# Four turned value tiles keep their store buffer in dead rows of the start stage instead of the result ring

## The chip, the core and the metric

The kernel runs on one core of one Trainium2 chip. The metric is the device time of one execution in microseconds (us). Matrix products run on TensorE (PE in the profile), vector work on VectorE (DVE), casts and activations on ScalarE (ACT), small work and a part of the transfers on GpSimd (POOL). SyncE (SP) only issues transfers.

## The reference, cut to what matters

One decoder layer on 1024 tokens with 1024 channels: a normalised and modulated input `h`, one wide projection, windowed attention and a gated recurrence side by side, and a merge.

```
h = rmsnorm(x, norm_g) * (1 + scale) + shift
proj = h @ w_in
q_a, k_a, v_a, z_a, q_b, f_b, i_b, z_b, g_a, g_b = split(proj)
o_a = dilated_attention(heads(q_a), heads(k_a), heads(v_a), rel_bias) * silu(z_a)   # 8 heads of 64
o_b = rmsnorm(hgrn2(silu(q_b), f_b, i_b, lb)) * silu(z_b)
y = sigmoid(g_a) * (o_a @ w_branch_a) + sigmoid(g_b) * (o_b @ w_branch_b)
out = rmsnorm(x + gate * (y @ w_out), final_g)
```

The change touches the values `v_a` of heads 2 and 3. The projection leaves them with channels on partitions; attention wants them with tokens on partitions.

## The kernel before

Every product is split in three (high by high, low by high, high by low part); `mm3` (L240 to L243) records the three matmuls. `split` (L245) makes the parts of a weight piece: a cast on ACT (`w_hi`, L248) and a difference on DVE (`w_lo`, L226).

**The stream.** The projection is a list of steps, each of which prepares one piece of weights (128 x 4 x 128 floats, 256 KB) and runs twelve matmuls on it. Two column blocks together are done as seven products of sums of blocks (`add_pair`): the steps in order take the pieces `i11`, a sum, a second sum, a third sum, `i12`, a difference, `i22`. A step's parts are prepared two steps ahead (`AHEAD`). The attention of head 0 begins while the stream still runs; its score and value steps are put between the products.

**The pieces.** Each piece is loaded by SP (L260) into one of eight slots, `w_raw0` to `w_raw7`. Slots 6 and 7 belong to a pool (`wraw2`) that opens only when the start stage has closed; they lie where the start stage had `xt0`. A slot gets a new piece when the old one has been split.

**The ring.** Results wait for their stores in a ring of six tiles `ct` of 128 x 512 (`ctile`, pool `ctp`). A seventh tile must wait until the store of an earlier one has landed.

**The turned values.** `ev_v(p)` takes the values of heads 2p and 2p+1 out of PSUM into a `ct` and, two or three steps later, turns them: PE transposes four blocks into `pt` (L452), ACT casts the high part into a `ct` (L456), DVE subtracts to get the low part (L226), and SP stores the tile (L458) to `vq_d` in memory. Each p has two halves of tokens and two tiles in each, so four stores of 256 KB. p = 0 and p = 1 are turned close together, where the start stage ends.

**The attention's loads.** POOL loads a head's half of `toep`, `qp`, `k1`, `k2` (L903, L909) and its turned values `vq` (L914). In head 0 the second half's loads are held back by four one-element copies on POOL (L901, L902) that read the last turned tile of p = 0.

**What sets the order.** PE's order is that of the code. ACT, DVE and POOL follow the code up to `region.close()`; behind it, and on SP throughout, the scheduler places an instruction by when what it needs is free in its plan. Each engine then works strictly in its order. `start` (with the input blocks `xt0` and `xt1` of 128 x 8 x 512) lies on the right of the on-chip memory; when it closes, the attention's tiles take its place.

Of the kernel before, what the change touches and what calls it, by code (L numbers as in the profile page):

```python
# [10 lines left out]
F32 = mybir.dt.float32  # L11
F32R = mybir.dt.float32r
# [7 lines left out]
P = 128  # L20
S = 1024
D = 1024
KT = D // P
# [156 lines left out]
def hybrid_layer(ctx: ExitStack, tc: tile.TileContext, x, w_ada, b_ada, w_in, w_branch_a, w_branch_b, w_out,  # L180
                 rel_bias, final_g, smalls, consts, onehot, logc, out, tap=None):
    nc = tc.nc
    ctx.enter_context(tc.manual_schedule(engines={mybir.EngineType.PE}))

    cpool = ctx.enter_context(tc.tile_pool(name="cpool", bufs=1))
# [14 lines left out]
    nc.gpsimd.memset(ones, 1.0)  # L200
    ident = kc[:, K_ID:K_ID + P]
    lbt = cpool.tile([P, 6, 8], F32, name="lbt")
    mx_, e0, e1, lb, oml, tm = (lbt[:, n] for n in range(6))


# [19 lines left out]
    def sub(out_, a, hi):  # L225
        nc.vector.tensor_tensor(out_, a, hi.bitcast(F32), ALU.subtract)  # L226
# [37 lines left out]
    def ctile(dt=F32):  # L264
        return ctp.tile([P, 512], dt, name="ct")
# [123 lines left out]
    def half_of(th):  # L389
        return slice(512 * th, 512 * th + 512)  # L390

    def as_ct(src, psum):
        if not psum:
            return src
        t = ctile()
        nc.scalar.copy(t, src)
        return t
# [42 lines left out]
    def ev_k(p):  # L440
        return ev_split(4 * p + 2, 1.0)

    turned, last_v = {}, {}

    def ev_v(p, wait=2):
        def ev(src, th, psum):
            t = as_ct(src, psum)

            def turn():
                pt = pools["t"].tile([P, 4, P], F32, name="pt")  # L450
                for n in range(4):
                    nc.tensor.transpose(pt[:, n], t[:, n * P:(n + 1) * P], ident)  # L452
                for n in (0, 2):
                    vs = ctile(F32R).rearrange("p (a h e) -> p a h e", a=2, h=2)
                    got = pt[:, n:n + 2].rearrange("p a (h e) -> p a h e", h=2)
                    nc.scalar.copy(vs[:, :, :, 0:E], got)  # L456
                    sub(vs[:, :, :, E:P], got, vs[:, :, :, 0:E])
                    nc.sync.dma_start(vq_d[p][:, 4 * th + n:4 * th + n + 2], vs.bitcast(F32))  # L458
                    last_v[p] = vs
                turned["v", p] = turned.get(("v", p), 0) + 1  # L460
            stream.after(wait, turn)
        return ev
# [58 lines left out]
    with ExitStack() as st:  # L521
        px = st.enter_context(tc.tile_pool(name="ps_x", bufs=1, space=PSUM))
        pm = st.enter_context(tc.tile_pool(name="ps_main", bufs=1, space=PSUM))
        xt = [sp.tile([P, KT, 512], F32, name=f"xt{th}") for th in range(2)]
# [141 lines left out]
        def first_products(j, ths=(0, 1), us=(0, 1, 2)):  # L666
            for th in ths:
                bh, bl = X[NAMES[j // 4, th]]
                k = j % 4
                for u in us:  # L670
                    hi, lo = firsts[u + 3 * (j // 4)]
                    nc.tensor.matmul(main[u, th], hi[:, k], bh[:, k], start=j == 0, stop=False)
                    nc.tensor.matmul(main[u, th], lo[:, k], bh[:, k], start=False, stop=False)
                for u in us:
                    nc.tensor.matmul(main[u, th], firsts[u + 3 * (j // 4)][0][:, k], bl[:, k], start=False,
                                     stop=j == KT - 1)

        def block_sum(name, c):

            s, u = slice(2 * c, 2 * c + 2), slice(2 * c + 4, 2 * c + 6)  # L680
            to, a, b_ = {"t1": (xt[0][:, s], xt[1][:, s], xt[0][:, s]), "t3": (xt[1][:, s], xt[1][:, u], xt[1][:, s]),
                         "t2": (xt[0][:, s], xt[1][:, u], xt[0][:, s]),
                         "t4": (xt[0][:, u], xt[0][:, u], xt[0][:, s])}[name]
            hi, lo = X[name]
            return [lambda: nc.vector.tensor_tensor(to, a, b_, ALU.subtract),
                    lambda: nc.scalar.copy(hi[:, s], to), lambda: sub(lo[:, s], to, hi[:, s])]
# [4 lines left out]
        def tick(another=True):  # L691

            if sums and another:
                under_way.append(block_sum(*sums.pop(0)))
            for parts in under_way:
                parts.pop(0)()
            while under_way and not under_way[0]:
                under_way.pop(0)
# [142 lines left out]
        tick()  # L841
        first_products(KT - 1, us=(0,))
        stream.ahead(0, 1)
        tick()
        for th in range(2):
            FIRST[0][1](main[0, th], th, True)
# [25 lines left out]
    with ExitStack() as at:  # L872
# [7 lines left out]
        def load_head(h):  # L880
            p = h // 2
            if p > 0:
                stream.need(f"qk{p}")
            while turned.get(("v", p)) != 2:
                stream.step()
            qp, k1, k2 = ([ap1.tile([P, 512], F32R, name=f"{n}{c}") for c in range(2)] for n in ("qp", "k1", "k2"))
            toep = ap1.tile([P, S], F32, name="toep")
            heads[h] = qp, k1, k2, toep, [None, None]
            load_half(h, 0)
            if h == 0:  # L890
                load_half(h, 1)
            load_value(h, 0)

        def load_half(h, c):


            qp, k1, k2, toep, _ = heads[h]
            if h == 0 and c == 1:
                got = last_v[0][:, 0, 0, 0:1].bitcast(F32)
                for t in (qp[1], k1[1], k2[1]):  # L900
                    nc.gpsimd.tensor_copy(t[:, 0:1], got)  # L901
                nc.gpsimd.tensor_copy(toep[:, 512:513], got)  # L902
            nc.gpsimd.dma_start(toep[:, half_of(c)],  # L903
                                bass.AP(tensor=toep_d.tensor, offset=toep_d.offset + h * TOEP + 512 * c,
                                        ap=[[1, P], [1, 512]]))
            p, r = h // 2, slice(E * (h % 2), E * (h % 2) + E)
            for dst, n in ((qp, 4 * p), (k1, 4 * p + 2), (k2, 4 * p + 3)):
                for hh in range(2):
                    nc.gpsimd.dma_start(dst[c][E * hh:E * hh + E],  # L909
                                        qk_d[n + hh if dst is qp else n][r, half_of(c)].bitcast(F32R))  # L910
# [60 lines left out]
        def begin(n):  # L971

            if n < len(items):
                h, j = items[n]
                rows[n] = []
                for i in (2 * j, 2 * j + 1):
                    rows[n].append(score(h, i))
                    if i == 1:
                        if h > 0:
                            load_half(h, 1)  # L980
                        load_value(h, 1)
                    if i == 7 and h + 1 < NH:
                        load_head(h + 1)
                    yield
# [519 lines left out]
```

## Time and profile before

| what | us |
|---|---|
| median of three executions (1118.89 to 1120.88) | 1120.68 |
| profiled execution, its own time | 1119.58 |
| its span, first to last instruction | 1117.70 |
| PE busy | 1093.9 |
| DVE busy | 807.4 |
| ACT busy | 554.9 |

Times in the views are counted from the first instruction. The start of a row and its duration overlap with the next row's, since instructions are pipelined; what matters is the distance from start to start. The place of this change lies between 83 us (where the first transposes of values stand) and 119 us.

### The profile page before, as it was taken

How to read it: one execution, taken by the hardware profiler on the slowest of the kernel's cores; microseconds unless marked ns; L12 is line 12 of the kernel's file. 1: busy time of each engine (PE TensorE's matmuls, PEld its weight loads, DVE VectorE, ACT ScalarE, POOL GpSimd, SP SyncE). 2: the span in 40 equal slices, each digit the busy share in tenths (PEclk: the TensorE clock that was granted, in tenths of full speed). 3: DMA queues.
4: the chain of work that ended last, by engine and by line, in shares of the span. 5: the costliest groups of instructions: out<-in, count | busy, mean ns of one | idle time of the engine just before them, and what ended most of it. 6: DMA issues, size and time to landing. Idle time of an engine off the chain costs nothing.

```text
span 1117.7 us, 21827 instructions
## 1 busy us (share of the span) xinstructions
PE 1093.9 (98%) x8302; PEld 905.0 (81%) x8302; DVE 807.4 (72%) x1607; ACT 554.9 (50%) x1144; POOL 124.0 (11%) x207
## 2 busy tenths in 40 slices
PE   8998999999999999999999999999999999999997
PEld 6687888888888888888887888878887888888886
DVE  5586988878777776854788898897977773769053
ACT  6564656687555555632455554555554443334021
POOL 1112202203203201100000000000010012000000
PEclk9999999999999999999999999999999999999999
DMA  9849567637636624856625354453534379854052
GB/s 311 265 126 244 170 180 189 175 104 179 161 102 169 156 73 148 268 164 211 225 86 180 104 191 129 137 165 92 188 124 154 130 263 351 267 187 138 13 189 75
DMA packets 161608, 189.54 MB, mean 170 GB/s; under 512 B 11440, under 2 KB 107824, under 8 KB 161504
## 3 DMA queue, kind: packets, MB, share of 16 engines
q1 hardware_dynamic: 140080, 153.95, 43.1%
q0 software_dynamic: 21024, 33.60, 12.3%
q8 instruction: 65, 1.06, 0.4%
q10 hardware_dynamic: 400, 0.61, 0.2%
q14 instruction: 39, 0.32, 0.1%
HBM read 129.36 MB, written 58.76 MB: 168 GB/s over the span
## 4 chain that ended last, share of the span: by engine, by line
PE 79%; DVE 8%; DMA 6%; issue 3%; ACT 2%; POOL 1%; DVEq 0%; POOLq 0%; SPq 0%; ACTq 0%
PE m L241 17%; PE m L243 16%; PE m L242 16%; PE po L959 3%; PE pt L944 3%; PE pq L241 3%; PE pq L243 2%; PE pq L242 2%; PE pp L1125 2%; DMA gbr<-gb_d 2%; DVE w_lo L226 2%; PE pss L927 1%; PE pss L926 1%; DMA ld<-in_w_ada_dram 1%; PE pou L1221 1%
## 5 line engine op out<-in xcount | busy, mean ns | idle before, releaser
L226 DVE TENSOR_TENSOR w_lo<-w_raw,w_hi 128x512 fp32r<-128x512 f32 x156 | 106.9, 687 | 59.4 <-ACT w_hi L248 59.0
L248 ACT CAST w_hi<-w_raw 128x512 fp32r<-128x512 f32 x146 | 90.5, 621 | 43.7 <-PE m L243 29.2
L248 ACT CAST w_hi<-w_s 128x512 fp32r<-128x512 f32 x90 | 55.9, 621 | 56.6 <-PE m L243 37.9
L330 ACT COPY ct<-m 128x512 f32<-128x512 f32 x90 | 52.7, 585 | 58.4 <-PE m L243 48.8
L277 DVE TENSOR_TENSOR ct<-m,ct 128x512 f32<-128x512 f32 x90 | 61.8, 687 | 23.9 <-PE m L243 23.6
L226 DVE TENSOR_TENSOR w_lo<-w_s,w_hi 128x512 fp32r<-128x512 f32 x90 | 61.8, 687 | 11.7 <-ACT w_hi L248 10.6
L932 ACT ACTIVATE s<-s,st 128x128 f32<-128x128 f32 (+3 forms) x64 | 49.8, 778 | 33.0 <-DVE st L929 33.0
L948 ACT CAST pth<-pt 128x512 fp32r<-128x512 f32 (+1 forms) x80 | 43.5, 544 | 34.0 <-PE pt L944 29.7
L1229 POOL TENSOR_TENSOR ssh<-ssh,halfh 128x4 f32<-128x4 f32 x16 | 19.5, 1216 | 332.9 <-DVE ssh L1228 332.8
L226 DVE TENSOR_TENSOR ptl<-pt,pth 128x512 fp32r<-128x512 f32 (+1 forms) x80 | 50.6, 632 | 7.4 <-ACT pth L948 6.6
L241 PE MATMUL m<-t3h,w_hi 128*128 128x512 f32 x120 | 49.5, 412 | 2.2 <-ACT w_hi L248 2.2
L241 PE MATMUL m<-b22h,w_hi 128*128 128x512 f32 x124 | 50.9, 410 | 0.0
L241 PE MATMUL m<-b11h,w_hi 128*128 128x512 f32 x124 | 50.9, 410 | 0.0
L241 PE MATMUL m<-b21h,w_hi 128*128 128x512 f32 x124 | 50.6, 408 | 0.0
L241 PE MATMUL m<-t4h,w_hi 128*128 128x512 f32 x120 | 49.5, 412 | 1.1 <-issue 0.5
L242 PE MATMUL m<-b22h,w_lo 128*128 128x512 f32 x124 | 48.6, 392 | 1.8 <-issue 1.8
L241 PE MATMUL m<-t2h,w_hi 128*128 128x512 f32 x120 | 49.2, 410 | 0.7 <-ACT ct L330 0.7
L241 PE MATMUL m<-t1h,w_hi 128*128 128x512 f32 x120 | 49.4, 412 | 0.3 <-DVE ct L277 0.3
L243 PE MATMUL m<-b21l,w_hi 128*128 128x512 f32 x124 | 48.6, 392 | 0.0
L242 PE MATMUL m<-b11h,w_lo 128*128 128x512 f32 x124 | 48.6, 392 | 0.0
L243 PE MATMUL m<-b11l,w_hi 128*128 128x512 f32 x124 | 48.6, 392 | 0.0
L243 PE MATMUL m<-b22l,w_hi 128*128 128x512 f32 x124 | 48.6, 392 | 0.0
(365 smaller groups left out, 3226.6 us busy)
## 6 DMA issues: line engine op xcount, KB each, us to landing
w_raw<-in_w_in_dram SPq DMA_DIRECT2D x128, 256.0 KB, 3.5
wa<-in_w_ada_dram SPq DMA_DIRECT2D x16, 512.0 KB, 9.2
qk_d<-ct SPq DMA_DIRECT2D x32, 256.0 KB, 3.1
k<-qk_d POOLq DMA_DIRECT2D x64, 128.0 KB, 5.2
toep<-toep_d POOLq DMA_DIRECT2D x16, 256.0 KB, 5.5
qp<-qk_d POOLq DMA_DIRECT2D x32, 128.0 KB, 5.1
vq_d<-ct SPq DMA_DIRECT2D x16, 256.0 KB, 3.9
vq<-vq_d POOLq DMA_DIRECT2D x16, 256.0 KB, 4.3
```

Source lines behind the costliest of these rows:

```text
L226: nc.vector.tensor_tensor(out_, a, hi.bitcast(F32), ALU.subtract)
L241: nc.tensor.matmul(ps, ah, bh, start=start, stop=False, skip_group_check=more)
L242: nc.tensor.matmul(ps, al, bh, start=False, stop=False, skip_group_check=more)
L243: nc.tensor.matmul(ps, ah, bl, start=False, stop=stop, skip_group_check=more)
L248: nc.scalar.copy(hi, src)
L277: nc.vector.tensor_tensor(out_, a, b_, op)
L330: nc.scalar.copy(c[name], b[which])
L932: nc.scalar.activation(s[:, :kw], s[:, :kw], AF.Exp, bias=prev, scale=-1.0, accum_out=st2[:, 2:3])
L944: nc.tensor.transpose(pt[:, c0:c0 + P], pn[b][:, kt * P:(kt + 1) * P], ident)
L948: nc.scalar.copy(pth[:, :w], pt[:, :w])
L959: nc.tensor.matmul(po[:, 256 - n:256], vq[kt // 4][:, kt % 4], src[:, c0:c0 + n], start=kt == 0 and a == 0, stop=kt == 2 * j + 1 and a == 1)
L1125: nc.tensor.matmul(to[:, 0], k_[:, o:o + 32], q_[:, o:o + 32], start=True, stop=True)
```

## The change

The four tiles of p = 1 (heads 2 and 3) are no longer `ct` tiles. They use rows 4 to 7 of `xt1`, the second half's input block, which nothing reads any more at that place. And the element that POOL's four copies read is first copied to a tile of its own, `came`, by one DVE instruction, so that the ring tile isn't read by POOL.

```diff
+    came = cpool.tile([P, 16], F32, name="came")[:, 0:1]
...
                 for n in (0, 2):
-                    vs = ctile(F32R).rearrange("p (a h e) -> p a h e", a=2, h=2)
+                    vs = vs_free.pop(0).bitcast(F32R) if p == 1 else ctile(F32R)
+                    vs = vs.rearrange("p (a h e) -> p a h e", a=2, h=2)
...
-                    last_v[p] = vs
+                    if p == 0 and (th, n) == (1, 2):
+                        nc.vector.tensor_copy(came, vs[:, 0, 0, 0:1].bitcast(F32))
...
         stream.ahead(0, 1)
+        vs_free.extend(xt[1][:, n] for n in range(4, KT))
...
-                got = last_v[0][:, 0, 0, 0:1].bitcast(F32)
                 for t in (qp[1], k1[1], k2[1]):
-                    nc.gpsimd.tensor_copy(t[:, 0:1], got)
-                nc.gpsimd.tensor_copy(toep[:, 512:513], got)
+                    nc.gpsimd.tensor_copy(t[:, 0:1], came)
+                nc.gpsimd.tensor_copy(toep[:, 512:513], came)
```

The lines behind the first edit move by one to four. PE's order is the same before and after. On the other engines rows move. A tile's number at its end counts up in the program; the same piece has a number smaller by two in the changed program (`w_raw7_976` before is `w_raw7_974` after: slot 7, the piece `i11` with which the next pair of column blocks begins).

On SP, from the last stores of the first keys on, before:

```order
L260 DMA w_raw6_974<-in_w_in_dram 128x4x128
L260 DMA w_raw7_976<-in_w_in_dram 128x4x128
L458 DMA vq_d_97<-ct_856 128x512
L458 DMA vq_d_97<-ct_860 128x512
L458 DMA vq_d_97<-ct_869 128x512
L458 DMA vq_d_97<-ct_873 128x512
L458 DMA vq_d_97<-ct_922 128x512
L458 DMA vq_d_97<-ct_926 128x512
L458 DMA vq_d_97<-ct_935 128x512
L458 DMA vq_d_97<-ct_939 128x512
L260 DMA w_raw2_982<-in_w_in_dram 128x4x128
L260 DMA w_raw3_984<-in_w_in_dram 128x4x128
```

and after, at the same place:

```order
L460 DMA vq_d_98<-ct_857 128x512
L460 DMA vq_d_98<-ct_861 128x512
L460 DMA vq_d_98<-ct_870 128x512
L460 DMA vq_d_98<-ct_874 128x512
L460 DMA vq_d_98<-xt1_119 128x512 x4
L261 DMA w_raw2_980<-in_w_in_dram 128x4x128
L261 DMA w_raw3_982<-in_w_in_dram 128x4x128
L261 DMA w_raw4_984<-in_w_in_dram 128x4x128
L261 DMA w_raw6_972<-in_w_in_dram 128x4x128
L261 DMA w_raw7_974<-in_w_in_dram 128x4x128
```

The two loads of slots 6 and 7 stood ahead of all eight stores and now stand behind them, as the last of five loads; the load of slot 7 also waits for the first store out of `xt1` to have landed, the third of the five waits for the DVE low part of slot 4 (`w_lo_961<-w_raw4_603`).

On DVE, where the pieces of the running pair are used up and the first scores of head 0 begin, before:

```order
L226 TENSOR_TENSOR w_lo_944<-w_raw2_598,w_hi_943 128x512
L277 TENSOR_TENSOR w_raw4_602<-w_raw3_600,w_raw4_602 128x512
L929 ISA s0_1028,st2_1029<-pss_1030,toep_1007 128x128
L929 ISA st2_1029 128x1
L226 TENSOR_TENSOR w_lo_963<-w_raw4_602,w_hi_962 128x512
L933 RECIPROCAL st2_1029<-st2_1029 128x1
L929 ISA s0_1043,st2_1044<-pss_1045,toep_1007 128x256
```

and after:

```order
L278 TENSOR_TENSOR w_raw4_603<-w_raw3_601,w_raw4_603 128x512
L227 TENSOR_TENSOR w_lo_961<-w_raw4_603,w_hi_960 128x512
L278 TENSOR_TENSOR w_raw0_976<-w_raw7_974,w_raw0_976 128x512
L227 TENSOR_TENSOR w_lo_1062<-w_raw7_974,w_hi_1061 128x512
L933 ISA s0_1026,st2_1027<-pss_1028,toep_1005 128x128
L933 ISA st2_1027 128x1
L937 RECIPROCAL st2_1027<-st2_1027 128x1
L938 TENSOR_SCALAR s0_1026<-s0_1026,st2_1027 128x128
L933 ISA s0_1041,st2_1042<-pss_1043,toep_1005 128x256
```

Two operations on slot 7 (`w_raw7_974`) now stand ahead of the first score's minimum (`s0_1026<-pss`), where before it needed no load of that kind.

On ACT, at the same place, before:

```order
L248 CAST w_hi_943<-w_raw2_598 128x512
L330 COPY ct_959<-m2_882 128x512
L248 CAST w_hi_962<-w_raw4_602 128x512
L932 ACTIVATE s0_1028,st2_1029<-s0_1028,st2_1029 128x128
L248 CAST w_hi_1063<-w_raw7_976 128x512
```

and after:

```order
L249 CAST w_hi_941<-w_raw2_599 128x512
L331 COPY ct_957<-m2_884 128x512
L249 CAST w_hi_960<-w_raw4_603 128x512
L249 CAST w_hi_1061<-w_raw7_974 128x512
L936 ACTIVATE s0_1026,st2_1027<-s0_1026,st2_1027 128x128
```

The cast of slot 7 changed places with the first exponential of head 0. On POOL the four copies now read `came`, and the first load of turned values (`vq`) moved from behind the second half's seven loads of `toep`, `qp` and `k` to ahead of them.

More of the change, by code (lines that the diff above doesn't have):

```diff
@@ L441, in ev_k @@
         return ev_split(4 * p + 2, 1.0)
-    turned, last_v = {}, {}
+    turned, vs_free = {}, []
     def ev_v(p, wait=2):
```

## The prediction

> **What bounds the kernel now.** I read the page first.
>
> ```profile
> span 1117.7 us, 21827 instructions
> PE 1093.9 (98%) x8302; PEld 905.0 (81%) x8302; DVE 807.4 (72%) x1607; ACT 554.9 (50%) x1144; POOL 124.0 (11%) x207
> ```
>
> PE is busy for all but 24 us, so only time in which PE stands still, or starts again late, can be won or lost. Next the chain that ended last, between 60 and 126 us (start, length, what):
>
> ```profile
> 90.92 0.59 ACT ct L330
> ...
> 93.83 7.71 DMA vq_d<-ct
> 101.65 0.59 ACT ct L330
> ...
> 118.65 0.38 PE pss L926
> ```
>
> and the waits between 80 and 125 us (us in total, times, longest):
>
> ```profile
> ACT ct L330 <- DMA vq_d<-ct: 4.9, 1, 4.9
> PE m L241 <- ACT w_hi L248: 2.2, 1, 2.2
> ACT ct L456 <- DMA vq_d<-ct: 1.8, 2, 1.5
> PE m L241 <- ACT ct L330: 0.7, 1, 0.7
> ```
>
> The copy of a product into the ring at 101.65 waits for the fifth store of turned values (the first of heads 2 and 3), which takes 7.71 us to land. From there the chain goes over ACT and DVE, and is back on PE only at 118.65. PE's timeline prices the stall (start, length, [idle before it]):
>
> ```profile
> 83.46 1.03 PE L452 MATMUL pt<-kc,ct 128*128 128x128 f32 x8
> 84.25 0.48 PE L241 MATMUL m<-b11h,w_hi 128*128 128x512 f32 x1
> 89.81 1.04 PE L452 MATMUL pt<-kc,ct 128*128 128x128 f32 x8
> 91.56 0.50 PE L241 MATMUL m<-t2h,w_hi 128*128 128x512 f32 x1 [0.71 <-ACT ct L330]
> 100.18 0.39 PE L243 MATMUL m<-b21l,w_hi 128*128 128x512 f32 x1
> 102.81 0.49 PE L241 MATMUL m<-t3h,w_hi 128*128 128x512 f32 x1 [2.24 <-ACT w_hi L248]
> 106.20 0.49 PE L944 MATMUL pt<-kc,s 128*128 128x128 f32 x3
> ...
> 114.43 0.48 PE L926 MATMUL pss<-k,qp 128*128 128x512 f32 x1
> ```
>
> **What the change removes.** Two PE stalls. First, the eight transposes at 83.46 are followed by the next product after 0.79 us; those at 89.81 only after 1.75 us, because the copy at 90.92 waits for the first store to land. SP's queue shows why that is late:
>
> ```profile
> 86.02 0.94 SPq L260 DMA_DIRECT2D w_raw<-in_w_in_dram  x2
> 87.06 9.97 SPq L458 DMA_DIRECT2D vq_d<-ct  x8
> 97.50 6.37 SPq L260 DMA_DIRECT2D w_raw<-in_w_in_dram  x3
> ...
> vq_d<-ct SPq DMA_DIRECT2D x1, 256.0 KB, 3.8
> ```
>
> (The last row is the issue list of 87 to 87.3 us: the first store takes 3.8 us, so it lands at 90.9.) With the two loads of 86.02 gone from ahead of it, it goes out some 0.7 us earlier and alone, and the product follows at 89.81 + 0.79 = 90.60: 0.96 us won. Second, the product that ends at 100.41 (100.18 and the 0.23 from one start to the next) would be followed at once by the twelve matmuls on t3, 12 x 0.23 = 2.75 us, which now end at 106.20: 106.20 - 100.41 - 2.75 = 3.04 us won, since the ring copy no longer waits for a store of heads 2 and 3. Together 4.0: PE would come to the transposes of the first scores (L944) at 102.2 and not at 106.20.
>
> **What it adds in work.** The copy to `came` is one DVE instruction on one column; nearest is a reciprocal of one column, 0.15 us (below). It stands ahead of the sums that feed the product at 90.6, whose low part has about 0.3 us to spare, so I take 0, and 0.15 at most. POOL's four copies begin after it instead of after the cast, half a us later. The `vq` load that now leads POOL's queue has to wait for two stores; what it delays, the second half of `qp` and `k`, is first used by the scores at 114.43. I take 0 for both.
>
> **What it moves, and the new wait.** The load of slot 7 is the last of five, and ahead of the first score DVE now has two operations on it, ACT one. Both engines work in order. So both stop until that load has landed (call this L), and PE stops at L944, whose input is the normalised first score. DVE and ACT rows for what must follow L:
>
> ```profile
> 96.26 0.42 DVE L226 TENSOR_TENSOR ct<-pt,ct 128x256 fp32r<-128x256 f32 x1 [0.44 <-ACT ct L456]
> 96.78 0.69 DVE L226 TENSOR_TENSOR w_lo<-w_raw,w_hi 128x512 fp32r<-128x512 f32 x1
> 97.39 0.69 DVE L277 TENSOR_TENSOR w_raw<-w_raw,w_raw 128x512 f32<-128x512 f32 x1
> 97.99 0.28 DVE L929 CUSTOM_DVE_ANT_0 s<-pss,toep 128x128 f32<-128x128 f32 x1
> 102.78 0.69 DVE L226 TENSOR_TENSOR w_lo<-w_raw,w_hi 128x512 fp32r<-128x512 f32 x1 [4.50 <-ACT w_hi L248]
> 103.39 0.15 DVE L933 RECIPROCAL st<-st 128x1 f32<-128x1 f32 x1
> 103.47 0.40 DVE L929 CUSTOM_DVE_ANT_0 s<-pss,toep 128x256 f32<-128x256 f32 x1
> 105.86 0.34 DVE L934 TENSOR_SCALAR s<-s,st 128x256 f32<-128x256 f32 x1
> ...
> 102.65 0.40 ACT L932 ACTIVATE s<-s,st 128x128 f32<-128x128 f32 x1
> 104.08 0.51 ACT L932 ACTIVATE s<-s,st 128x256 f32<-128x256 f32 x1
> ```
>
> After L: difference and low part 0.6 each (96.78 to 97.39 to 97.99), minimum 0.3, exponential with its sum 0.5, reciprocal and scaling 0.45, second minimum 0.4, second exponential 0.6, reciprocal and scaling 0.5, and some 0.25 between engines: 4.2 us. L944 starts at L + 4.2 against 106.20, a difference of L - 102.0. DVE's order then still holds two operations of 0.6 (a low part and a scaled result) that before were done by 106.2; as the chain runs over DVE until 118.65, PE gets its next free run 1.2 us later still, a difference of L - 100.8. I take the middle, L - 101.4. Behind 118.65 the chain is PE alone, so the difference stays to the end.
>
> **How late is L?** From below: the third of the five loads waits for the DVE low part of slot 4. Before, DVE's last turned value is done at 96.7; the casts waited 1.8 us for stores, of which some 1.2 come off, since DVE's other work stands between: 95.5, followed by cast and low part of slot 2 (1.2), the difference and cast of slot 4 (1.0) and its low part (0.6): 98.3. Two more issues at 0.4 each put the last load at 99.1, and the fastest landing in this stretch was 2.9:
>
> ```profile
> DMA to landing us min/median/max: 2.9/3.8/8.9
> DMA to landing us min/median/max: 7.9/8.4/8.9
> 90.00:92.00 2.00, 1.29 (x10) 1.01 (x9) 1.02 (x2) 1.08 (x3) 2.00 (x5) 1.00 1.08 340
> q0 software_dynamic: 390, 0.52, 109.7%
> ```
>
> (First row: loads of pieces, 80 to 125 us. Second: the two of them issued at 97.50 and 98.10. Third: the stretch 90 to 92 us, its last number GB/s. Fourth: the only queue that moved data from 94.3 to 96.5 us.) So L is at least 102.0. From above: the two loads issued at 97.50 and 98.10 sat behind four stores and beside POOL's loads and landed after 7.9 and 8.9 us, at 105.4 and 107.0. In the changed kernel two loads stand at that place too, issued within a us of it, and three more follow. At 340 GB/s 256 KB take 0.77 us, three 2.3: L = 109.3. Between these lies the wait of the last load for the first store out of `xt1`: if that lands like its predecessor, at 93.83 + 7.71 = 101.5, the load goes out then, and with nothing ahead of it lands at 101.5 + 0.4 + 2.9 = 104.8. I take 109, because the row of loads behind the same four stores is the nearest. The sum is 109 - 101.4 = 7.6 us slower: 1119.58 + 7.6 = 1127.2 for the profiled execution, and from the median, which lies 1.10 above it, 1128.3.
>
> [...]
>
> **The clock.** PE would stand still from 102.2 to 113. Before, it stood still in parts of 20 to 24 us:
>
> ```profile
> 20.00:24.00 4.00, 2.32 (x9) 1.16 (x10) 2.50 (x7) 3.30 (x6) 0.00 (x0) 0.98 1.02 402
> 24.00:28.00 4.00, 4.00 (x11) 2.76 (x11) 3.96 (x11) 3.48 (x7) 0.17 (x1) 0.59 1.08 357
> ```
>
> The granted clock (third from the end) then was 0.59 for 4 us, a loss of up to 0.41 x 4 = 1.6 us. After the new stall DVE leads, so I take 0 and keep 1.6 for the upper end. [...]
>
> **Rivals.** (1) *The queue drains sooner.* The two early loads are no longer in the way, POOL's loads start later, and only the wait for the first `xt1` store counts: L between 103.5 and 106, about 104.8, and the sum is 3.4, a time of 1124.1. [...] Against it: 7.9 and 8.9 us in the same place. (2) *The load is nearly in time.* L between 102.0 and 103.5: between 0.6 and 2.1 slower, about 1122.0, the stall of the ring paid back by the stall of the load. It needs the first `xt1` store to land by about 99, in 5.5 us, where its predecessor took 7.71. (3) *Faster.* If the last load landed by 98, before DVE needs it, nothing is left but the relief: 4.0 us won, 1116.7. It decides at L = 101.4 and shows beyond noise at 99.2. It needs the third load to be released some 3 us earlier than 98.3; the casts and differences ahead of it, 0.6 each, hardly leave that. A kernel of this kind can be told from an unchanged one by about 0.2%, 2.2 us.
>
> **How the numbers follow.** Last of a full queue (L from 106 to 111): 0.63. Rival 1: 0.21. Rival 2: 0.09. Rival 3: 0.07. The forecast is the first, 1128.3. Slower by over 0.2% (L above 103.6) is the first two, 0.84; within 0.2% rival 2, 0.09; faster 0.07. For the range, L = 102.8 gives 1.4 and 1122.0 at the lower end; L = 110.5 with the clock's 1.6 gives 10.7 and 1131.4 at the upper, which leaves out rival 3, most of rival 2 and a few in a hundred above.
>
> **What would show it.** In the changed kernel: no ACT ring copy (L331) waits for a store near 101; PE's product after the second eight transposes starts near 90.6 and the t3 product ends near 102; then DVE's difference of slot 7 (L278) and ACT's cast (L249) wait for a `w_raw` load until about 109, and PE's transposes of scores (L948) start some 4 us later, with a lower granted clock behind them. I am wrong if that load lands by 102, or if DVE and PE catch up behind the stall.

## The result and the profile after

The changed kernel takes 1125.66 us (median of five, 1123.59 to 1126.79) against 1119.93 for the kernel before in the same runs (1116.81 to 1120.88): a ratio of 1.0052, 95% interval 1.0037 to 1.0066, so 5.7 us slower. The prediction was 1128.3, range 1122.0 to 1131.4. The profiled execution shown here took 1124.04 us. Where the diff added lines, a line's number has moved by one to four (L226 is L227, L277 is L278, L926 is L930, L944 is L948).

The page, and the waits between 80 and 125 us (us in total, times, longest):

```profile
span 1122.2 us, 21825 instructions
PE 1094.3 (98%) x8302; PEld 906.5 (81%) x8302; DVE 807.6 (72%) x1608; ACT 554.8 (49%) x1144; POOL 124.1 (11%) x207
```

```profile
ACT w_hi L249 <- DMA w_raw<-in_w_in_dram: 9.1, 1, 9.1
PE pt L948 <- DVE s L938: 8.4, 2, 7.3
DVE w_raw L278 <- DMA w_raw<-in_w_in_dram: 8.3, 1, 8.3
```

PE's busy time is the same to 0.4 us, and the span grew by 4.5. No ring copy waits for a store any more. In its place ACT and DVE wait for one load of a weight piece, and PE waits for DVE. The chain that ended last says which load (start, length, what):

```profile
99.76 0.50 SPq L261
...
100.31 6.69 DMA w_raw<-in_w_in_dram
...
107.08 0.63 ACT w_hi L249
```

It is the last of five, and it landed at 107.0. PE's timeline (start, length, [idle before it]):

```profile
83.68 1.04 PE L453 MATMUL pt<-kc,ct 128*128 128x128 f32 x8
...
90.03 1.03 PE L453 MATMUL pt<-kc,ct 128*128 128x128 f32 x8
90.81 0.48 PE L242 MATMUL m<-t2h,w_hi 128*128 128x512 f32 x1
...
99.59 0.39 PE L242 MATMUL m<-t3h,w_hi 128*128 128x512 f32 x1
...
102.09 0.39 PE L244 MATMUL m<-t3l,w_hi 128*128 128x512 f32 x1
109.82 0.45 PE L948 MATMUL pt<-kc,s 128*128 128x128 f32 x1 [7.35 <-DVE s L938]
111.29 0.69 PE L948 MATMUL pt<-kc,s 128*128 128x128 f32 x2 [1.02 <-DVE s L938]
...
124.59 0.38 PE L930 MATMUL pss<-k,qp 128*128 128x256 f32 x1
```

Both stalls of the ring are gone: the products on t2 and t3 follow without a gap. PE gets to the score transposes (L948) at 102.3, and stands there until 109.82.

To compare the place alone, and not what the start stage or the later stages do in one execution or another, I use one distance from here on, D: from the first eight transposes of values to the score product 256 wide that ended the chain before (83.46 to 118.65 in the kernel before: 35.19 us). Here it is 124.59 - 83.68 = 40.91, which is 5.72 more, as much as the medians differ (5.73).

### The profile page after: what moved, and what is told of

The parts are those of the page before. It is cut to its first block, busy times and chain, and to the rows that moved or that the text cites. A ratio compares the mean times of both kernels' runs of the same rounds, so it can differ in the third digit from the quotient of the medians.

```text
span 1122.2 us, 21825 instructions
## 1 busy us (share of the span) xinstructions
PE 1094.3 (98%) x8302; PEld 906.5 (81%) x8302; DVE 807.6 (72%) x1608; ACT 554.8 (49%) x1144; POOL 124.1 (11%) x207
## 4 chain that ended last, share of the span: by engine, by line
PE 87%; DVE 6%; DMA 2%; issue 2%; ACT 2%; POOL 1%; SPq 0%; POOLq 0%; DVEq 0%; ACTq 0%
PE m L242 18%; PE m L244 17%; PE m L243 17%; PE pq L242 4%; PE pq L243 4%; PE pq L244 4%; PE po L963 3%; PE pt L948 3%; PE pp L1129 2%; PE pss L931 2%; PE pss L930 2%; PE pou L1225 1%; PE pm L675 1%; PE pm L678 1%; PE pou L1210 1%
## 5 line engine op out<-in xcount | busy, mean ns | idle before, releaser
L227 DVE TENSOR_TENSOR w_lo<-w_raw,w_hi 128x512 fp32r<-128x512 f32 x156 | 106.8, 686 | 57.7 <-ACT w_hi L249 57.2
L278 DVE TENSOR_TENSOR ct<-m,ct 128x512 f32<-128x512 f32 x90 | 61.8, 686 | 22.8 <-PE m L244 22.5
L227 DVE TENSOR_TENSOR w_lo<-w_s,w_hi 128x512 fp32r<-128x512 f32 x90 | 61.8, 687 | 11.6 <-ACT w_hi L249 10.5
L227 DVE TENSOR_TENSOR ptl<-pt,pth 128x512 fp32r<-128x512 f32 (+1 forms) x80 | 50.5, 631 | 7.3 <-ACT pth L952 6.5
L948 PE MATMUL pt<-kc,s 128*128 128x128 f32 x288 | 45.2, 274 | 8.4 <-DVE s L938 8.4
L948 PEld LDWEIGHTS pt<-kc,s 128*128 128x128 f32 x288 | 36.0, 141 | 18.9 <-issue 7.7
```

Of the source, the lines that this page charges most:

```text
L278: nc.vector.tensor_tensor(out_, a, b_, op)
L948: nc.tensor.transpose(pt[:, c0:c0 + P], pn[b][:, kt * P:(kt + 1) * P], ident)
```

## The experiments

L is the landing of slot 7, read as the start of DVE's difference on it (L278); each kernel's L is also given from its own first transposes of values. The column at the right is D less that. Each ratio comes from its own comparison and isn't just the quotient of the medians; the kernel before had medians of 1118.99 to 1119.93 beside the several runs, so two medians from different comparisons can differ by up to 0.9 us for that alone. Except for the wait without the relief, each edit below is shown against the changed kernel.

| kernel | median us | ratio to before, interval | L, and from the transposes | D | D - L |
|---|---|---|---|---|---|
| before | 1119.93 | | not waited for | 35.19 | |
| the change | 1125.66 | 1.0052 (1.0037 to 1.0066) | 107.02, 23.34 | 40.91 | 17.57 |
| `came` alone | 1118.19 | 0.9982 (0.9968 to 0.9995) | not waited for | 35.02 | |
| rows of xt1 alone | 1126.11 | 1.0051 (1.0035 to 1.0067) | 106.45, 23.06 | 41.31 | 18.25 |
| the change, load early | 1115.23 | 0.9946 (0.9926 to 0.9966) | not waited for | 32.36 | |
| 28 matmuls in the stall | 1124.40 | 1.0036 (1.0021 to 1.0051) | 106.32, 23.28 | 41.58 | 18.30 |
| 52 matmuls in the stall | 1125.31 | 1.0053 (1.0033 to 1.0073) | 106.70, 23.60 | 41.89 | 18.29 |
| the wait without the relief | 1124.17 | 1.0039 (1.0021 to 1.0057) | 105.41, 21.82 | 39.86 | 18.04 |
| POOL held by copies | 1128.36 | 1.0089 (1.0074 to 1.0104) | 111.02, 27.38 | 44.94 | 17.56 |
| POOL's loads later | 1123.07 | 1.0032 (1.0019 to 1.0045) | 104.70, 21.27 | 39.17 | 17.90 |
| load early, eight tiles in xt1 | 1115.20 | 0.9964 (0.9948 to 0.9981) | not waited for | 31.91 | |
| load early, no `came` | 1116.39 | 0.9971 (0.9955 to 0.9988) | not waited for | 32.33 | |

**The two edits apart.** First `came` alone; the turned tiles stay in the ring:

```diff
-                    vs = vs_free.pop(0).bitcast(F32R) if p == 1 else ctile(F32R)
+                    vs = ctile(F32R)
```

> The kernel before with the one-column copy `came` alone: POOL's four small copies read `came` and not the ring tile; the turned values of heads 2 and 3 stay in the ring, and the two loads of pieces stay ahead of the stores. My theory (the loss is the late load of slot 7, which the rows of xt1 bring): the time of before, within 0.15%, both stalls of the ring copies (0.71 and 2.24 us in front of the products on t2 and t3) still there, no wait for slot 7. Rival (the loss comes from the copy, or from POOL starting its loads later): 2 us or more slower than before.

```profile
82.89 1.03 PE L453 MATMUL pt<-kc,ct 128*128 128x128 f32 x8
...
102.06 0.50 PE L242 MATMUL m<-t3h,w_hi 128*128 128x512 f32 x1 [1.69 <-ACT w_hi L249]
...
117.91 0.39 PE L930 MATMUL pss<-k,qp 128*128 128x256 f32 x1
```

The stall before t3's product is still there, 1.69 us for 2.24, and D is 35.02, 0.17 less than before. The median fell by 1.4 us, which is more than D tells; the expectation of 0.15% was just missed, and where the rest comes from is open. Then the rows alone; POOL reads the ring tile as before:

```diff
                     if p == 0 and (th, n) == (1, 2):
-                        nc.vector.tensor_copy(came, vs[:, 0, 0, 0:1].bitcast(F32))
+                        last_v.append(vs)
...
+                came = last_v[0][:, 0, 0, 0:1].bitcast(F32)
```

> The change without `came`: the turned values of heads 2 and 3 go to the rows of xt1, and POOL's four small copies read the last tile of heads 0 and 1 in the ring, as before. My theory: as the whole change, 5 to 6 us slower than before (1125 to 1126); the load of slot 7 lands at about 107 and PE's transposes of scores start some 4.3 us after it. If the copy's release of POOL's loads half a us later mattered to SP's loads, slot 7 would land at least 0.5 us later or earlier than 107.0. Rival (`came` carries the loss): the time of before or better.

1126.11, 0.1 above the expected 1125 to 1126: the rows carry the whole loss. Slot 7 landed at 106.45, 0.57 us sooner than in the change, or 0.28 if both are counted from the transposes. Only the first of these passes the 0.5 us of the expectation, so an effect of `came` on SP's loads isn't shown. D is 0.40 above the change.

**The load in time.** xt0 gets a pool of its own, closed first, and the pool of slots 6 and 7 opens before xt1 is given back:

```diff
+        xt[0] = stx0.enter_context(tc.tile_pool(name="start0", bufs=1, side="right")).tile([P, KT, 512], F32, name="xt0")
...
-    stx.close()
+    stx0.close()
     stream.more = ctx.enter_context(tc.tile_pool(name="wraw2", bufs=1, reuse_waits="tile"))
     stream.issue()
+    stx.close()
```

> The whole change, but xt0 has a pool of its own that is closed first, so that the last two slots' loads (w_raw6, w_raw7) can go into xt0's place and stand ahead of all eight stores in SP's queue, as they did before the change; xt1 is given back after. The order of DVE's and ACT's work is that of the change: the work on slot 7 still stands ahead of the first score. My theory: slot 7 has landed long before DVE comes to it (by about 95), PE comes to the transposes of the first scores 3 to 4 us earlier than before, no half clock near 105, and the time is 2.5 to 4 us below before (1116 to 1117.5), 8 to 10 below the change. Rival A (the order of DVE's and ACT's work is the loss, not the load): 2 to 6 us slower than before, as the change. Rival B (the relief is not worth anything further on, because DVE leads until the second half's scores): within 1 us of before.

```profile
83.23 1.04 PE L453 MATMUL pt<-kc,ct 128*128 128x128 f32 x8
...
91.67 0.50 PE L242 MATMUL m<-t2h,w_hi 128*128 128x512 f32 x1 [1.05 <-ACT ct L331]
...
103.20 0.49 PE L950 MATMUL pt<-kc,s 128*128 128x128 f32 x3
...
115.59 0.39 PE L932 MATMUL pss<-k,qp 128*128 128x256 f32 x1
```

No stall in front of the transposes of scores, which start at 103.20 (106.20 before); the stall before t2 stays, since two loads again stand ahead of the first store. DVE's low part and ACT's cast of slot 7 stand ahead of the first score here as in the change, so that order by itself doesn't bring the loss: rival A fell, and rival B too. (DVE's difference on slot 7 is back at its old place, at 93.83 against 93.72 in the kernel before. It stood ahead of the first score in that kernel as well; the low part and the cast are what the change brought ahead of it.) At 1115.23 this version is faster than both kernels, and 0.8 below the range expected. D is 2.83 less than before; the medians differ by 4.4, and what lies beyond D I can't place.

**The clock.** In the change the granted clock fell while PE stood (start and end, PE busy; third from the end the clock, last GB/s):

```profile
100.00:104.00 4.00, 2.48 (x11) 1.70 (x10) 0.00 (x0) 0.00 (x0) 0.00 (x0) 1.00 1.28 285
104.00:108.00 4.00, 0.00 (x0) 0.00 (x0) 0.96 (x2) 0.62 (x1) 0.00 (x0) 0.57 0.50 129
108.00:112.00 4.00, 1.16 (x4) 0.89 (x5) 3.30 (x12) 2.44 (x7) 0.00 (x0) 0.50 0.00 0
112.00:116.00 4.00, 4.00 (x13) 3.31 (x13) 3.90 (x7) 2.00 (x5) 0.95 (x2) 0.65 0.61 199
```

On seeing this I took some 1.5 us of the loss for the clock's, against the prediction's 0, and tried it:

```diff
+            for _ in range(28 if (h, j, m) == (0, 0, 0) else 0):
+                nc.tensor.matmul(pt, heads[0][0][0][:, 0:P], heads[0][1][0][:, 0:512], start=True, stop=True)
```

> The whole change, with 28 more matmuls of 128x512 on PE (6.2 us of work, written into the tile of the first transposes and overwritten by them) in the stall ahead of the first scores' transposes, so that PE is busy while it waits. My theory on the clock (of the 5.7 us, about 1.5 come from the half clock that was granted from 104.6 to 114.9): the granted clock stays near 1.0 there, slot 7 still lands near 107 and the transposes still start 4.3 us after it, and the time is 1.0 to 1.5 us below the change (about 1124.3). Rival (DVE's chain leads behind the stall and hides the clock, as the prediction had it): the clock stays up and the time is that of the change within 0.3 us.

The half clock only moved: 0.58 in the stretch from 112 to 116. D is 41.58 and not less than in the change, though the median is 1.3 lower, which left it open. So PE was kept busy throughout:

```diff
+            for _ in range(34 if warm else 0):
...
+                    if warm and (kk, b) == (0, 1):
+                        for _ in range(18):
```

> The changed kernel with PE kept busy through the whole stall: 34 added matmuls of 128x512 (7.7 us of work) ahead of the first scores' first transpose, and 18 of 128x128 between it and the second. With 28 alone the half clock had only come later (0.58 in the stretch 112 to 116), and the gain over the changed kernel was gone by 124 us. Theory A (DVE's chain leads behind the stall, the clock costs little): the clock stays 1.0 from 100 to 124, PE then waits for DVE between 114 and 124, and PE's lead over the changed kernel at 124 to 140 us is under 0.5 us once the difference in the start stage is taken off; the time is that of the run with 28 matmuls, 1124 to 1125.5. Theory B (the clock costs 1.5 us of its own): PE leads the changed kernel by 1.2 to 1.6 us at 140 us, and the time is 1123.5 to 1124.5.

```profile
108.00:112.00 4.00, 4.00 (x31) 3.62 (x30) 3.30 (x12) 2.65 (x7) 0.00 (x0) 1.00 0.00 0
112.00:116.00 4.00, 4.00 (x19) 3.34 (x18) 3.87 (x8) 1.75 (x4) 1.08 (x2) 1.00 0.86 216
116.00:120.00 4.00, 3.23 (x14) 2.22 (x13) 3.58 (x11) 2.23 (x7) 0.00 (x0) 1.00 0.88 275
```

```profile
119.52 0.30 PE L955 MATMUL pt<-kc,s 128*128 128x128 f32 x1 [0.59 <-DVE s L938]
120.46 0.55 PE L955 MATMUL pt<-kc,s 128*128 128x128 f32 x3 [0.64 <-DVE s L938]
```

The clock was 1.00 and the time 1125.31, that of the change. What PE won it gave back in two waits for DVE, 0.59 and 0.64. Theory A holds: DVE leads behind the stall, and the half clock costs nothing that these runs can show. (DVE's order also moved a little in these two, and the 18 matmuls held the second transposes up by some 0.5 us, so D - L is 0.7 above the change's; a gain of 1.5 would show all the same.)

**Do relief and wait add up?** The kernel before, ring and all, with the wait for a store out of xt1 alone:

```diff
+                    if p == 1 and (th, n) == (0, 0):
+                        nc.vector.tensor_copy(xt[1][:, 4, 0:16], vs[:, 0, 0, 0:16].bitcast(F32))
+                        nc.sync.dma_start(late_d, xt[1][:, 4, 0:16])
```

> The kernel before, ring and all, with the wait of the change alone: the first turned tile of heads 2 and 3 has 16 columns copied to xt1 and from there stored (8 KB), so that the last two slots' loads have to wait for that store and stand behind the stores on SP, as in the change. The relief of the ring is thus left out. My theory (once PE has to wait for slot 7, what it won ahead of that is lost, so the difference is L - 101 whatever the relief): slot 7 lands between 106 and 109, PE comes to the first scores' transposes 4.3 us after, the ring's stall of over 2 us is still there in front of t3's product and costs nothing, and the time is that of the change within 2 us (1125 to 1128). Rival (relief and wait add up): 4 us more than the change, 1129 to 1131.

```profile
98.45 0.50 PE L242 MATMUL m<-b21h,w_hi 128*128 128x512 f32 x1 [1.50 <-ACT w_hi L249]
...
108.15 0.45 PE L948 MATMUL pt<-kc,s 128*128 128x128 f32 x1 [3.47 <-DVE s L938]
```

```profile
105.41 0.69 DVE L278 TENSOR_TENSOR w_raw<-w_raw,w_raw 128x512 f32<-128x512 f32 x1 [3.84 <-DMA w_raw<-in_w_in_dram]
```

They don't. The ring's stall is there (1.50 us, before the product on b21 this time), and the time is 1124.17, 1.5 below the change and not 4 above it (0.8 below if each is taken from its own kernel before). D is 1.05 below the change. Slot 7 stands second of its five loads here and lands 1.6 us sooner (105.41 against 107.02). From issue to landing its load took as long as in the change, 6.66 us for 6.69, so those 1.6 us are its earlier issue, at 98.73 and not 100.31:

```profile
98.73 6.66 DMA w_raw<-in_w_in_dram
```

I had put the landing at 106 to 109 and the time at 1125 to 1128, so they were missed by 0.6 and 0.8 us.

**What makes L.** Six copies on POOL ahead of its loads for the second half, to hold 1 MB back from the DMA engines:

```diff
                     nc.gpsimd.tensor_copy(t[:, 0:1], came)
+                    for _ in range(2):
+                        nc.gpsimd.tensor_copy(t, X["b11"][0][:, 0])
```

> The changed kernel with POOL held up: six copies of 128x512 (into the second half's tiles of qp and k, which the loads overwrite) stand ahead of POOL's loads of toep, qp and k for the second half of head 0 (1 MB in all), so that these are issued some us later than 91 and only after SP's stores of heads 2 and 3. It tells what the landing of slot 7 (107.0 in the change) is made of. Theory A (the 16 DMA engines are full from 92 to 107, and transfers of both queues are served in the order of issue, so that the last load lands when what was issued ahead of it is through): SP's four stores in rows of xt1 land by about 97, the last load 2 to 3 us earlier, at 104 to 105, and as DVE works without a gap from that landing on, the time is 2 to 3 us below the change, 1122.5 to 1124. Theory B (the load is late because of when it is issued, after 100, and of its own wait for a store): it lands within 0.7 us of 107, and the time is that of the change.

Both theories missed; it took 1128.36. The added work itself got in the way (first row: this kernel; second: the same operation in the change):

```profile
92.36 2.55 DVE L227 TENSOR_TENSOR w_lo<-w_s,w_hi 128x512 fp32r<-128x512 f32 x1 [0.69 <-ACT w_hi L249]
```

```profile
92.10 0.69 DVE L227 TENSOR_TENSOR w_lo<-w_s,w_hi 128x512 fp32r<-128x512 f32 x1 [0.69 <-ACT w_hi L249]
```

With POOL copying beside it, the difference took 2.55 us and not 0.69, SP's stores came 2.5 us later, and slot 7 landed at 111.02, 4.00 us later than in the change: its load was issued 2.5 us later, at 102.83, and took 1.5 us longer, 8.16. D grew by 4.03: one us of L was one us of D. The same 1 MB was then held back without work, by letting POOL's four copies read the first normalised score:

```diff
-            if h == 0:
-                load_half(h, 1)
...
-                    nc.gpsimd.tensor_copy(t[:, 0:1], came)
+                    nc.gpsimd.tensor_copy(t[:, 0:1], rows[0][0][:, 0:1])
...
                     rows[n].append(score(h, i))
+                    if n == 0 and i == 0:
+                        load_half(0, 1)
```

> The changed kernel with POOL's loads of toep, qp and k for the second half of head 0 (1 MB) held back until the first normalised score is there: the four one-element copies read that score and not `came`. No added work on any engine this time: in the run before, POOL's six copies had stretched DVE's operations, the stores came 2.5 us later, slot 7 landed at 111.0 and PE was 4.0 us behind the change, so neither theory was tested. Theory A (DMA engines full from 92 to 107, both queues served in the order of issue): with 1 MB less ahead of it, at 340 GB/s, slot 7 lands 3 us earlier, at 103.5 to 104.5, PE's first transposes of scores start 4.3 us after it, and the time is 2.5 to 3.5 us below the change (1122 to 1123.3), unless the second half's loads, now late, are waited for at 116 to 120. Theory B (the load is late because of when it is issued and of its own wait for a store): it lands within 0.7 us of 107, the time is that of the change.

```profile
99.44 5.24 DMA w_raw<-in_w_in_dram
```

```profile
100.00:104.00 4.00, 2.23 (x10) 1.50 (x8) 0.00 (x0) 0.00 (x0) 0.00 (x0) 1.00 0.85 245
```

Slot 7 landed 2.3 us sooner, at 104.7, and the time is 1123.07, 2.6 below the change (D is 1.74 below). Of the 2.3 us, 0.9 are an earlier issue, at 99.44 and not 100.31, and 1.4 a shorter way from issue to landing, 5.24 us and not 6.69. So both theories have a part: what stands in the DMA engines ahead of the load counts, as theory A has it, though not by its full 3 us, and so does the time of its issue. In this stretch (the row above) the DMA engines moved 245 GB/s at a share of 0.85, against 285 at 1.28 in the change, so they were no longer full all through.

**Can the version with the load early be bettered?** All eight turned tiles in rows of xt1:

```diff
-                    vs = vs_free.pop(0).bitcast(F32R) if p == 1 else ctile(F32R)
+                    vs = vs_free.pop(0).bitcast(F32R) if p < 2 else ctile(F32R)
...
-        vs_free.extend(xt[1][:, n] for n in range(4, KT))
+        vs_free.extend(xt[1][:, n] for n in range(KT))
```

> The version with xt0 in a pool of its own, with all eight turned tiles, those of heads 0 and 1 too, in rows of xt1, so that no ring copy can wait for a store of turned values. Theory: the one stall that was left, 1.05 us in front of the product on t2 (the ring copy waited for the first store, which stood behind two loads), goes, PE comes to the first scores 0.8 to 1.0 us earlier, and the time is 0.5 to 1.0 us below that version (1114.3 to 1114.8). Rival (DVE leads from there, or the next wait of the ring takes its place): within 0.3 us of it.

```profile
101.73 0.49 PE L950 MATMUL pt<-kc,s 128*128 128x128 f32 x3
...
110.11 0.30 PE L950 MATMUL pt<-kc,s 128*128 128x128 f32 x1 [0.92 <-DVE st L939]
```

The stall of 1.05 us goes and the first scores' transposes start 1.3 us sooner from the transposes of values on, but 0.92 of it comes back as a wait for DVE, and D is only 0.45 shorter. The median is the same, 1115.20: the rival. Last, the version with the load early without `came` (the edit as in the rows alone):

> The version with xt0 in a pool of its own, without the one-column copy `came`: POOL's four copies read the last ring tile of heads 0 and 1 themselves, and start about half a us earlier. If the copy is free, as the prediction took it, the time is that of that version within 0.1% (1114 to 1116.3). If the later start of POOL's loads is what made the copy alone 1.4 us faster than the kernel before (the stores then landed 0.7 us earlier), this is 0.7 to 1.5 us slower (1116 to 1116.7).

D is 32.33 against 32.36, so the copy is worth nothing at this place, one way or the other. The median is 1.2 higher all the same, as the second reading forecast. Differences of 1 to 1.5 us between medians without one in D turned up here, in `came` alone and with the 28 matmuls. Whether the copy gains something elsewhere in the kernel is open.

## Why the prediction was right, and where it was off

**The relief, 4.0 us.** Right. The product on t2 starts 0.78 us after the transposes in front of it (90.03 to 90.81; forecast 0.79), t3's runs to 102.3 (forecast 102.2). And it is not paid out, as the formula had it: left out, it changed D - L by no more than the kernels differ among themselves (18.04, in a range of 17.56 to 18.30).

**The cost of `came`, 0.** Right at this place: D fell by 0.17 with the copy alone, and by 0.03 when it was taken away from the version with the load early.

**The wait, L - 101.4.** Right in kind and size. In the change DVE takes up slot 7 at 107.02 and the second row's transposes, on which the next scores wait, start at 111.29, 4.3 later, for a calculated 4.2. The same two rows where slot 7 came sooner (POOL's loads later):

```profile
104.70 0.69 DVE L278 TENSOR_TENSOR w_raw<-w_raw,w_raw 128x512 f32<-128x512 f32 x1 [6.26 <-DMA w_raw<-in_w_in_dram]
```

```profile
108.97 0.69 PE L946 MATMUL pt<-kc,s 128*128 128x128 f32 x2 [1.02 <-DVE s L936]
```

Again 4.3. With L = 107.0 the two ends of the term, L - 102.0 and L - 100.8, give 5.0 and 6.2, and 118.65 became 124.59, 5.94 later (5.72 from the transposes of values on). Over seven kernels with L between 104.7 and 111.0, D - L lies between 17.56 and 18.30.

**L, 109.** This is the term that was mis-sized: it measured 107.0, and the 2.0 us are most of the 2.6 by which the time was overrated (the rest is mostly the kernel before, 1119.93 in these runs and 1120.68 in those the sum started from). The row taken as nearest, the two loads behind the same four stores that needed 7.9 and 8.9 us, did not carry over. The other wait that the prediction weighed, that of slot 7's load for the first store out of xt1, did not set L: the store landed at 97.7 (93.88 + 3.8), and the load went out only at 100.31. It was held up by its place in SP's order, behind the third load, which had to wait for DVE's low part of slot 4 until 98.7 (forecast 98.3, and 99.1 at the earliest for the last load). Rows of the changed kernel (SP's queue; its loads from issue to landing; the first store out of xt1, from issue to landing):

```profile
86.62 2.48 SPq L460 DMA_DIRECT2D vq_d<-ct  x4
93.88 2.38 SPq L460 DMA_DIRECT2D vq_d<-xt  x4
96.72 5.94 SPq L261 DMA_DIRECT2D w_raw<-in_w_in_dram  x5
```

```profile
DMA to landing us min/median/max: 6.4/6.7/7.2
```

```profile
vq_d<-xt SPq DMA_DIRECT2D x1, 256.0 KB, 3.8
```

The first store of heads 2 and 3 took 3.8 us and not 7.71, and the loads behind 6.4 to 7.2. POOL's part of the traffic had moved: its `vq` load now led, and the loads of the second half were issued some 2 us later (first rows: the change; the last: the kernel before), so part of them stood behind that store and not ahead of it. The two weight loads ahead of SP's first stores were gone as well. Two other runs tell these apart in part: with the two loads ahead, the first store of heads 2 and 3 took 6.9 us where POOL's loads began at 89.22 (`came` alone), and 4.9 us where they began at 91.98 (load early).

```profile
91.15 0.56 POOL L907 DMA_DIRECT2D toep<-toep_d  x1
...
92.73 2.11 POOL L913 DMA_DIRECT2D k<-qk_d  x4
```

```profile
89.29 0.57 POOL L903 DMA_DIRECT2D toep<-toep_d  x1 [0.30 <-POOL toep L902]
```

The prediction named both facts, `vq` leading and the later start, and costed them at nothing because no engine waits for those loads. Their effect on SP's transfers was not asked in the sum, only in rival 1, which named the two missing loads too. The run with POOL's loads held back shows it: the last of the five loads, that of slot 7, took 5.24 us there and not 6.69.

This is what the two queues moved from 94 to 96 us of the changed kernel and, below it, from 96 to 98 us (packets, MB, share):

```profile
q0 software_dynamic: 296, 0.49, 105.3%
q1 hardware_dynamic: 23, 0.05, 11.1%
```

```profile
q1 hardware_dynamic: 236, 0.44, 63.4%
q0 software_dynamic: 180, 0.28, 52.4%
```

SP's first store out of xt1 (queue q1) had been issued at 93.88, but from 94 to 95.5 us its queue moved one packet, while POOL's (q0) moved 231 packets, 0.39 MB. The first store of heads 0 and 1, issued at 86.62 with little else under way, had moved 0.02 MB by 87.5 us. In the kernel before, the store of 93.83 moved nothing before 96.5. So these two stores began to move some 1.6 and 2.7 us after their issue, and the store of 86.62 within 0.9 us. From 96 to 98 us of the changed kernel both queues moved at once, 0.44 and 0.28 MB. What made the two stores wait isn't shown, and neither is what sets the time from issue to landing in L.

**The clock, 0.** Right, though the profile after seems to say 1.5: with the clock kept at 1.00 the time was 1125.31 against 1125.66, since DVE leads, as the prediction argued.

**The rivals.** The time lay between the forecast and rival 1 (1124.1, L about 104.8). Rival 3's condition, the load in time, gave 1115.23 when it was made to hold, for a forecast of 1116.7. That they lie so close is partly chance: only one of the two stalls was gone there, and D fell by 2.83 and not by 4.0. Rivals 2 and 3 themselves did not come.

## What to carry to other kernels

When a buffer is moved to other memory, ask what the allocator wanted to put there next: here a block was borrowed for four stores, and the weight loads that had stood ahead of the stores in SP's order were placed behind them. That place made the load of slot 7 late, and not the wait itself: the store it had to wait for had landed 2.6 us before it went out. A wait removed ahead of a later one was worth nothing here; look for the last wait before the engine that sets the end, and price only that one (here D was L, both from the same start, plus 17.6 to 18.3, whatever was won ahead of it). And ask what else is under way when a late transfer goes out, on the other queue too: with 1 MB held back on POOL's queue, SP's load landed 2.3 us sooner here, 0.9 of it by an earlier issue and 1.4 by a shorter way to landing.

## What the runs showed of the hardware

Beside POOL's copies of 128x512 a DVE difference of 128x512 took 2.55 us, and 0.69 in the change. The rows don't show what held it up.

The granted clock also fell after two short stalls. With 28 matmuls in the gap PE stood for 0.81 and 1.24 us only, 2.05 together, and the clock was then 0.58 over 4 us:

```profile
109.04 0.33 PE L950 MATMUL pt<-kc,s 128*128 128x128 f32 x1 [0.81 <-DVE s L938]
110.60 0.44 PE L950 MATMUL pt<-kc,s 128*128 128x128 f32 x2 [1.24 <-DVE s L938]
```

```profile
112.00:116.00 4.00, 4.00 (x12) 3.15 (x11) 3.87 (x7) 2.12 (x4) 1.09 (x2) 0.58 0.83 218
```
